# Contracting products of both feed-forward parts by seven block products, token block by token block

## The chip, the cores and the metric

The kernel runs on one core of one Trainium2 chip. The metric is device time in microseconds (us) of one execution; the time shown is the median of three runs. The profile is of one further execution. Engines are named as in the profile: PE (TensorE matmul), PEld (its weight load), DVE (VectorE), ACT (ScalarE), POOL (GpSimd), SP (SyncE, which here only issues DMAs).

## The reference, cut to what matters

Three different blocks follow one another on 1024 tokens of width 1024, all in float32. The second and the third end in a feed-forward part, and only these are touched:

```
# second block; inner width 22 * 128 = 2816
hn = rmsnorm_2(h, norm_ffn)
g, up = split(hn @ w_ffn_in)
h = h + (silu(g) * up) @ w_ffn_out
return rmsnorm_2(h, norm_final)

# third block; inner width 32 * 128 = 4096
m = rmsnorm_3(h, norm_mlp_g) @ w_mlp_up
h = h + square(relu(m)) @ w_mlp_down
return rmsnorm_3(h, norm_final_g)
```

The change concerns the products with `w_ffn_out` and `w_mlp_down`, which contract over the inner width. They are called the down products here, those with `w_ffn_in` and `w_mlp_up` the up products.

## The kernel before

Activations stand with the feature in the partitions and the 1024 tokens along the row, as two halves h of 512 tokens. A unit is 128 features by 1024 tokens, 512 KB. Every product is done in three passes, to keep float32 accuracy: a matrix is split into a high part in the matmul's own number type (a cast on ACT, L158, or L76 for a whole weight unit) and the remainder (a subtraction on DVE, L159 or L77), and the three matmuls of `mm3` (L149 to L151) add high by high, high by low and low by high in one PSUM bank.

The up products already go by seven block products in place of eight (`block_gemm`, Winograd's form of Strassen's method): P1 to P7 are matmuls (L358) of sums and differences of weight blocks, which POOL makes (L330 to L335), and of token blocks B11, B21, B22, T1 to T4, which stand ready in 28 split pages. `operand` prepares the weights of a product up to six products ahead. The inner activations go to DRAM (`hid_d`) unit by unit.

The down products are plain. `down_loads` loads residual rows (`ur`) and inner units (`hraw`) from DRAM by POOL's DMA queue and splits each unit into two pages; `gemm_out` then takes a group of 2 or 4 units, and for each of the 16 output halves (eight column blocks m of 128, two token halves h) runs 3 matmuls a unit into one PSUM bank (`mm`), which DVE adds onto the residual rows (`ev_add`, L1252 in the second block, L1646 in the third). Groups are `FF_GROUPS` in the second block, eight times 4 units in the third. The last group of each block runs in `seam` or `final`, which go on into the norm that follows.

Weights come in `Weights`: a unit of 512 KB is loaded by SP's queue into one of two raw buffers (`wraw`, L65), split as a whole (L76, L77) into one of four `wsplit` buffers.

The scheduler of the language puts every engine's instructions into one fixed order, by readiness and program order; each engine then runs its own queue in that order, and a waiting instruction holds all behind it. A tile's buffer is given out again when its last reader is done. There are 28 general pages of 128x1024 (`page`), a second pool of pages (`xpage`: 8 in the second block and 3 extra, 11 in the third), 4 half pages for intermediate results (`half_tmp`), and eight PSUM banks (`mm` 2, `tp` 2, `sc` 2 of two banks each).

## Time and profile before

| | |
|---|---|
| median of three runs | 3386.79 us (3385.83 to 3386.85) |
| the profiled execution | 3385.71 us, span 3383.9 us, granted clock 0.987 |
| PE busy | 3266.0 us, 97% of the span |
| DVE, ACT, POOL busy | 1937.2, 1169.3, 510.2 us: 57%, 35%, 15% |
| second block | the up part's block products (L358) begin at 1638.3 us; additions of the down part (L1252) 2020.1 to 2275.1 us |
| third block | block products (L358) end at 3013.3 us; additions of the down part 3018.8 to 3323.4 us (L1646), in `final` 3326.1 to 3372.1 us (L1722) |

Busy is the union of the durations of an engine's instructions. Matmuls overlap in their pipeline, so the duration in a row is longer than the distance from one start to the next. Some records are missing in the trace, so counts in a stretch are a little low. The clock is that which the chip granted PE, as a share of full speed.

### The profile page before, as it was taken

The page shows a single profiled execution, that of the slowest core. Times are in us where ns is not written, and L with a number is a line of the kernel's source. Part 1 is how long each engine was busy: PE and PEld are TensorE (multiplying, and loading weights), DVE is VectorE, ACT ScalarE, POOL GpSimd, SP SyncE. Part 2 cuts the span into 40 slices and gives each one's busy share as a digit, 9 for nine tenths or more (in the row PEclk, how much of TensorE's full clock was granted, in tenths as well). Part 3 has the DMA queues.
Part 4 walks back from the last instruction along what each step waited for, and adds up shares of the span by engine and source line. Part 5 has one row for each costly group of instructions (what it writes and reads, how often), then busy time and mean ns, then how long its engine had stood idle before and what let it go on. Part 6 is the DMA issues. An engine that isn't in the chain of part 4 may idle for free. (4 is left out here: it accounts for less than half of the span.)

```text
span 3383.9 us, 41750 instructions
## 1 busy us (share of the span) xinstructions
PE 3266.0 (97%) x16039; PEld 2666.3 (79%) x16039; DVE 1937.2 (57%) x3619; ACT 1169.3 (35%) x2115; POOL 510.2 (15%) x461
## 2 busy tenths in 40 slices
PE   6999999999999999999999999999999989999998
PEld 6788877677777888887788877878878778878887
DVE  7465566664755562446755566455569765554444
ACT  5222344433444442213433342134443433332211
POOL 0000000002200000102423220040211243220002
PEclk9999999999999999999999999999999999999999
DMA  5133211322211244422122244121112233362211
GB/s 188 58 103 127 87 57 38 113 69 78 72 46 42 70 147 159 143 94 103 66 84 85 81 179 148 57 97 54 46 51 75 103 103 109 112 251 94 69 50 56
DMA packets 128632, 318.52 MB, mean 94 GB/s; under 512 B 16305, under 2 KB 34865, under 8 KB 128433
## 3 DMA queue, kind: packets, MB, share of 16 engines
q1 hardware_dynamic: 104976, 236.63, 20.5%
q0 software_dynamic: 21440, 76.51, 6.4%
q8 instruction: 126, 2.06, 0.3%
q10 hardware_dynamic: 2016, 2.72, 0.2%
q14 instruction: 74, 0.60, 0.1%
HBM read 232.90 MB, written 82.90 MB: 93 GB/s over the span
## 5 line engine op out<-in xcount | busy, mean ns | idle before, releaser
L149 PE MATMUL mm<-sp,wsplit 128*128 128x512 f32 (+1 forms) x2880 | 1151.0, 400 | 30.0 <-ACT sp L158 9.7
L150 PE MATMUL mm<-sp,wsplit 128*128 128x512 f32 (+1 forms) x2880 | 1132.4, 393 | 9.5 <-DVE sp L159 7.1
L151 PE MATMUL mm<-sp,wsplit 128*128 128x512 f32 (+1 forms) x2880 | 1129.7, 392 | 0.0
L149 PEld LDWEIGHTS mm<-sp,wsplit 128*128 128x128 f32 x2880 | 547.1, 190 | 149.2 <-ACT sp L158 14.1
L150 PEld LDWEIGHTS mm<-sp,wsplit 128*128 128x128 f32 x2880 | 548.5, 190 | 117.3 <-DVE sp L159 10.2
L151 PEld LDWEIGHTS mm<-sp,wsplit 128*128 128x128 f32 x2880 | 547.7, 190 | 111.4 <-issue 0.4
L358 PE MATMUL mm<-sp,wsplit 128*128 128x512 f32 x1632 | 390.5, 391 | 6.6 <-ACT scp L362 5.0
L76 ACT CAST wsplit<-wraw 128x1024 fp32r<-128x1024 f32 x196 | 205.7, 1049 | 494.3 <-PE mm L151 468.3
L358 PEld LDWEIGHTS mm<-sp,wsplit 128*128 128x128 f32 x1632 | 306.5, 188 | 73.5 <-ACT scp L362 5.4
L77 DVE TENSOR_TENSOR wsplit<-wraw,wsplit 128x1024 fp32r<-128x1024 f32 x196 | 244.8, 1250 | 152.7 <-ACT wsplit L76 145.1
L358 PE MATMUL sc<-sp,wsplit 128*128 128x512 f32 x1224 | 296.6, 391 | 1.3 <-DVE c L372 1.3
L358 PEld LDWEIGHTS sc<-sp,wsplit 128*128 128x128 f32 x1224 | 231.1, 189 | 51.0 <-DVE c L372 1.7
L190 POOL TENSOR_TENSOR acc<-acc,sqt 128x512 f32<-128x512 f32 (+1 forms) x105 | 140.1, 1346 | 474.9 <-ACT sqt L189 388.3
L1646 DVE TENSOR_TENSOR ur<-ur,mm 128x512 f32<-128x512 f32 x112 | 76.8, 686 | 152.1 <-PE mm L151 152.1
L159 DVE TENSOR_TENSOR wsplit<-ssum,wsplit 128x512 fp32r<-128x512 f32 x136 | 101.8, 750 | 89.1 <-ACT wsplit L158 88.9
L1252 DVE SCALAR_TENSOR_TENSOR ur<-mm,ur 128x512 f32<-128x512 f32 x96 | 66.2, 689 | 106.5 <-PE mm L151 106.3
L158 ACT CAST wsplit<-ssum 128x512 fp32r<-128x512 f32 x136 | 82.9, 621 | 109.8 <-POOL ssum L335 36.0
L158 ACT CAST sp<-hraw 128x512 fp32r<-128x512 f32 x108 | 64.0, 620 | 65.2 <-PE mm L151 44.1
L333 POOL TENSOR_TENSOR ssum<-ssum,wraw 128x512 f32<-128x512 f32 x34 | 51.9, 1527 | 221.7 <-DVE wsplit L159 221.7
L158 ACT CAST wsplit<-wraw 128x512 fp32r<-128x512 f32 x102 | 61.8, 620 | 67.4 <-PE sc L358 47.8
L159 DVE TENSOR_TENSOR sp<-hraw,sp 128x512 fp32r<-128x512 f32 x108 | 71.3, 686 | 11.6 <-ACT sp L158 11.6
L335 POOL TENSOR_TENSOR ssum<-wraw,ssum 128x512 f32<-128x512 f32 x34 | 47.3, 1390 | 196.9 <-DVE wsplit L159 196.9
(550 smaller groups left out, 4234.2 us busy)
## 6 DMA issues: line engine op xcount, KB each, us to landing
wraw<-W SPq DMA_DIRECT2D x264, 512.0 KB, 3.7
hraw<-hid_d POOLq DMA_DIRECT2D x54, 512.0 KB, 6.0
hid_d<-scp SPq DMA_DIRECT2D x68, 256.0 KB, 2.0
t_d<-gl SPq DMA_DIRECT2D x32, 256.0 KB, 2.0
u<-x_d POOLq DMA_DIRECT2D x16, 512.0 KB, 6.0
gl<-t_d POOLq DMA_DIRECT2D x32, 256.0 KB, 3.1
u_d<-u SPq DMA_DIRECT2D x32, 256.0 KB, 2.0
ur<-u_d POOLq DMA_DIRECT2D x16, 512.0 KB, 8.2
```

The lines of the kernel that those rows point to most:

```text
L76: K.nc.scalar.copy(s[:, 0, :], r)
L77: K.nc.vector.tensor_sub(s[:, 1, :], r, s[:, 0, :].bitcast(F32))
L149: t.matmul(ps, wh, xh, start=first, stop=False)
L150: t.matmul(ps, wh, xl, start=False, stop=False)
L151: t.matmul(ps, wl, xh, start=False, stop=last)
L158: nc.scalar.copy(hi, src)
L159: nc.vector.tensor_sub(lo, src, hi.bitcast(F32))
L190: eng.tensor_add(acc, acc, t[:, :acc.shape[-1]])
L333: nc.gpsimd.tensor_sub(s, s, a11)
L358: nc.tensor.matmul(d, wk[:, c, :], xk[:, e, :], start=new and k == y == 0, stop=k == 3 and y == 2, skip_group_check=not new)
L1252: nc.vector.scalar_tensor_tensor(uu(m, h), ps, 0.5, uu(m, h), op0=OP.mult, op1=OP.add)
L1646: nc.vector.tensor_add(uu(m, h), uu(m, h), ps)
```

## The change

The down products go by seven block products too. `block_down` takes groups of 6 or 8 inner units. In a group the lower and the upper half of the units are the two inner blocks, the two token halves the two token blocks, and a pair of column blocks (2p and 2p + 1, p from 0 to 3) the two output blocks. Its seven stages P2, P1, P5, P6, P3, P7, P4 run one after the other, each for the four pairs, so that 28 slots make a group; a slot is n/2 units by three matmuls (L521). Token blocks of a stage are split two stages ahead; T1 and T2 are made by DVE, T3 and T4 by POOL. Weights of a slot are prepared up to six slots ahead from half units which SP loads (L437), with sums and differences on POOL (L451 to L457). Stages P2, P5 and P3 use four banks (two `tp`, two `mm`), the others the four banks of `sc`. A slot of P2, P3, P7 and P4 is added onto the residual by DVE (L530); a slot of P1, P5 and P6, whose result serves two outputs, is copied by ACT to a half page (`ut`, L528) and added by POOL (L532), and the PSUM bank goes on being summed into. The first 18 of 22 and 28 of 32 units go this way (`DOWN_2`, `DOWN_3`); the last four stay in `seam` and `final`. `then` begins the loads for the down part five products before the up part ends (`res_loads`, `inner_load`); the plain group's units are loaded and split 42 slots before the end (`inner_parts`). The weights are laid out anew in DRAM by the host (`down_units`), with no arithmetic.

```diff
-FF_GROUPS = (2, 4, 4, 4, 4, 4)
+
+DOWN_2, DOWN_3 = (6, 6, 6, 4), (8, 8, 6, 6, 4)
...
+
+    def skip(self, n):
+
+        self.given = self.split = self.loaded = self.given + n
+        self.end = self.n
...
+            if j == len(seq) - 5:
+                then()
...
+    def res_loads(self, u, u_d, page):
+
+        for k in (0, 2, 4, 6, 1, 3, 5, 7):
+            u[k] = page(name="ur")
+            self.nc.gpsimd.dma_start(u[k], u_d[k])
+            if k % 4 == 2 or k % 4 == 3:
                 yield
...
+    def inner_load(self, hid_d, ms):
+        raw = []
+        for m in ms:
+            raw.append(self.page(name="hraw"))
+            self.nc.gpsimd.dma_start(raw[-1], hid_d[m])
+        return raw
+
+    def inner_parts(self, hid_d, hid, ms):
+
+        raw = self.inner_load(hid_d, ms)
+        yield
+        for m, r in zip(ms, raw):
+            for h in (0, 1):
+                t = hid[m, h] = self.split_page()
+                self.split(t, 0, 512, r[:, h * 512:h * 512 + 512])
+            yield
+
+    def block_down(self, groups, u, hid_d, pools, scale):
+
+
+        nc = self.nc
+        stages = (("P2", "B21"), ("P1", "B11"), ("P5", "T1"), ("P6", "T2"), ("P3", "B22"), ("P7", "T3"), ("P4", "T4"))
+        seq = [(g, st, p) for g in range(len(groups)) for st in range(7) for p in range(4)]
+        first = [sum(groups[:g]) for g in range(len(groups))]
+        base = self.W.given
+        loads = dict(P2=("12",), P1=("11",), P5=("21", "22"), P6=("11",), P3=("12",), P7=("11", "21"), P4=("22",))
+        cols = lambda g: groups[g] * 64
+        order = [(j, b) for j, (g, st, p) in enumerate(seq) for b in loads[stages[st][0]]]
+        got, put = {}, [0]
+
+        def load_to(j):
+            while put[0] < len(order) and order[put[0]][0] <= j:
+                i, b = order[put[0]]
+                if put[0] % 2 == 0:
+                    pool, tag = pools[put[0] // 2 % len(pools)]
+                    self.half = pool.tile([128, 1024], F32, name="wraw", tag=tag)
+                g, _, p = seq[i]
+                w = cols(g)
+                t = self.half[:, put[0] % 2 * 512:put[0] % 2 * 512 + w]
+                nc.sync.dma_start(t, self.W.ap[base + 8 * g + 2 * p + int(b[0]) - 1][:, (int(b[1]) - 1) * w:int(b[1]) * w])
+                got[i, b] = t
+                put[0] += 1
+        sums, wt = {}, []
+
+        def operand(j):
+            g, st, p = seq[j]
+            w = cols(g)
+            q = stages[st][0]
+            x = [got.pop((j, b)) for b in loads[q]]
+            if q == "P5":
+                if p % 2 == 0:
+                    sums[p] = self.page(name="ssum")
+                    sums[p + 1] = sums[p][:, 512:]
+                nc.gpsimd.tensor_add(sums[p][:, :w], x[0], x[1])
+            elif q == "P6":
+                nc.gpsimd.tensor_sub(sums[p][:, :w], sums[p][:, :w], x[0])
+            elif q == "P3":
+                nc.gpsimd.tensor_sub(sums[p][:, :w], x[0], sums[p][:, :w])
+            elif q == "P7":
+                nc.gpsimd.tensor_sub(x[0], x[0], x[1])
+            if j % 2 == 0:
+                wt.append(self.ws.tile([128, 2, 1024], F32R, name="wsplit"))
+            self.split(wt[-1], j % 2 * 512, w, sums[p][:, :w] if q in ("P5", "P6", "P3") else x[0])
+            return wt[-1], j % 2 * 512
...
+        def fetch(g, high):
+            if g < len(groups):
+                n = groups[g] // 2
+                for k, t in enumerate(self.inner_load(hid_d, range(first[g] + n * high, first[g] + n * high + n))):
+                    X[g, high, k] = t
+
+        def block(g, st, k):
+            if st > 6:
+                g, st = g + 1, st - 7
+            if g >= len(groups) or k >= groups[g] // 2:
+                return
+            b = stages[st][1]
+            lo, hi = X[g, 0, k] if (g, 0, k) in X else None, X[g, 1, k]
+            x11, x12 = (lo[:, :512], lo[:, 512:]) if lo is not None else (None, None)
+            x21, x22 = hi[:, :512], hi[:, 512:]
+            if b == "T1":
+                nc.vector.tensor_sub(x11, x12, x11)
+            elif b == "T2":
+                nc.vector.tensor_sub(x11, x22, x11)
+            elif b == "T3":
+                nc.gpsimd.tensor_sub(x12, x22, x12)
+            elif b == "T4":
+                nc.gpsimd.tensor_sub(x21, x21, x11)
+            t = B[g, st, k] = self.split_page()
+            self.split(t, 0, 512, dict(B21=x21, B11=x11, T1=x11, T2=x11, B22=x22, T3=x12, T4=x21)[b])
+        fetch(0, 1)
+        fetch(0, 0)
+        load_to(9)
+        yield
+        for st in (0, 1):
+            for k in range(4):
+                block(0, st, k)
+        a, f, ready = {}, {}, []
+        for j, (g, st, p) in enumerate(seq):
+            q = stages[st][0]
+            load_to(j + 10)
+            while len(ready) < min(j + 6, len(seq)):
+                ready.append(operand(len(ready)))
+            if p == 0 and st == 2:
+                fetch(g + 1, 1)
+            if p == 0 and st == 4:
+                fetch(g + 1, 0)
+            block(g, st + 2, p)
+            if q == "P2":
+                f[p] = (self.tp, self.tp, self.mm, self.mm)[p]()
+            elif q == "P1" and p % 2 == 0:
+                t = self.sc()
+                a[p], a[p + 1] = t[:, :512], t[:, 512:]
+            d = f[p] if q in ("P2", "P5", "P3") else a[p]
+            new = q in ("P2", "P1", "P5")
+            w, o = ready[j]
+            n = groups[g] // 2
             for k in range(n):
-                raw.append(pages[1](name="hraw"))
-                nc.gpsimd.dma_start(raw[k], hid_d[m + k])
-                yield
-            for k in range(n):
-                for h in (0, 1):
-                    t = self.split_page()
-                    self.split(t, 0, 512, raw[k][:, h * 512:h * 512 + 512])
-                    hid[m + k, h] = t
-                yield
-            m += n
+                xk = B[g, st, k]
+                wk = w[:, :, o + k * 128:o + k * 128 + 128]
+                for y, (c, e) in enumerate(((0, 0), (0, 1), (1, 0))):
+                    nc.tensor.matmul(d, wk[:, c, :], xk[:, e, :], start=new and k == y == 0, stop=k == n - 1 and y == 2,
+                                     skip_group_check=not new)
+            m, h = dict(P2=(0, 0), P1=(0, 0), P5=(1, 1), P6=(0, 1), P3=(0, 1), P7=(1, 1), P4=(1, 0))[q]
+            r = u[2 * p + m][:, h * 512:h * 512 + 512]
+            with self.tc.high_priority(offset=PRIO_E):
+                if q in ("P1", "P5", "P6"):
+                    t = self.half_tmp("ut")
+                    nc.scalar.activation(t, d, AF.Copy, scale=scale)
+                else:
+                    nc.vector.scalar_tensor_tensor(r, d, scale, r, op0=OP.mult, op1=OP.add)
+            if q in ("P1", "P5", "P6"):
+                nc.gpsimd.tensor_add(r, r, t)
+            yield
...
-        for _ in self.block_gemm(20, B, page, out):
+        hid = {}
+        n = sum(DOWN_2[:-1])
+        self.W.end = self.W.given + 40
+        down = self.block_down(DOWN_2[:-1], u2, hid_d, ((self.wr, "wraw"), (self.wr, "wraw")) + ((extra, "px"),) * 3, 0.5)
+
+        rl = []
+
+        def then():
+            next(down)
+            rl.append(self.spawn(self.res_loads(u2, u2_d, self.xpage)))
+        for _ in self.block_gemm(20, B, page, out, then):
             self.tick()
+        self.finish(*rl)
+        for i, _ in enumerate(down):
+            self.tick()
+            if i == 28 * len(DOWN_2) - 28 - 42:
+                self.W.skip(8 * len(DOWN_2) - 8)
+                mg = self.spawn(self.meta_norm())
+                dl = self.spawn(self.inner_parts(hid_d, hid, range(n, 22)))
+        self.finish(mg, dl)
+        self.x2_d = self.dr.tile([9, 128, 1024], F32, name="x2_d")
+        r = self.seam(u2, lambda k, h: hid[n + k, h], DOWN_2[-1], ev_add, "norm_final_2", "norm_mix_g_3", self.x2_d)
         px.close()
...
+        n = sum(DOWN_3[:-1])
+        self.W.end = self.W.given + 28
+        down = self.block_down(DOWN_3[:-1], u3, hid_d, ((self.wr, "wraw"), (self.wr, "wraw")) + ((self.px, "px"),) * 3, 1.0)
+
+        rl = []
+
+        def then():
+            next(down)
+            rl.append(self.spawn(self.res_loads(u3, u3_d, self.xpage)))
+        for _ in self.block_gemm(14, B, page, out, then):
             self.tick()
-        self.down = 0
-        self.spawn(self.down_loads(u3, u3_d, (self.page, self.xpage), hid, hid_d, (4,) * 8))
-        for gi in range(8):
-            m0 = 4 * gi
-            src3 = lambda k, h, m0=m0: hid[m0 + k, h]
-            self.down = gi
-            while (m0 + 3, 1) not in hid:
-                self.tick()
-            if gi < 7:
-                for _ in self.gemm_out(src3, 4, ev_add):
-                    self.tick()
-            else:
-                self.final(u3, src3)
+        self.finish(*rl)
+        for i, _ in enumerate(down):
+            self.tick()
+            if i == 28 * len(DOWN_3) - 28 - 42:
+                self.W.skip(8 * len(DOWN_3) - 8)
+                dl = self.spawn(self.inner_parts(hid_d, hid, range(n, 32)))
+        self.finish(dl)
+        self.final(u3, lambda k, h: hid[n + k, h])
...
+def down_units(w, groups):
+
+    out, o = [], 0
+    for i, n in enumerate(groups):
+        g = w[128 * o:128 * (o + n)]
+        o += n
+        if i + 1 < len(groups):
+            u = g.reshape(n, 128, 8, 128).transpose(2, 1, 0, 3).reshape(8, 128, n * 128)
+            out.append(np.concatenate([u, np.zeros((8, 128, 1024 - n * 128), w.dtype)], axis=2))
```

Two places show how the order of instructions moves. The first is POOL's queue in the second block, where the up part ends and the down part begins. `hraw` is a unit of inner activations, `ur` a residual row block; the rows with the names mtm, lrug and mtt load constants of the third block. Before:

```order
L335 TENSOR_TENSOR ssum<-wraw,ssum 128x512
L394 DMA hraw<-hid_d 128x1024 x2
L390 DMA ur<-u_d 128x1024 x6
L394 DMA hraw<-hid_d 128x1024 x2
L390 DMA ur<-u_d 128x1024
L394 DMA hraw<-hid_d 128x1024 x2
L1495 DMA mtm<-metat 16x512 x2
```

Now (`ssum` is a weight sum, `ut` a copied product):

```order
L342 TENSOR_TENSOR ssum<-wraw,ssum 128x512
L402 DMA hraw<-hid_d 128x1024 x6
L394 DMA ur<-u_d 128x1024 x7
L451 TENSOR_TENSOR ssum<-wraw 128x384 x3
L485 TENSOR_TENSOR hraw<-hraw 128x512 x3
L487 TENSOR_TENSOR hraw<-hraw 128x512
L451 TENSOR_TENSOR ssum<-wraw 128x384
L487 TENSOR_TENSOR hraw<-hraw 128x512
L394 DMA ur<-u_d 128x1024
L453 TENSOR_TENSOR ssum<-ssum,wraw 128x384 x2
L402 DMA hraw<-hid_d 128x1024 x3
L532 TENSOR_TENSOR ur<-ur,ut 128x512
```

The residual loads now come behind the first six units, and sums and differences stand between the loads where POOL had loads alone.

The second place is DVE's queue inside a down part of the second block. `sp` is a split page, `wsplit` a weight split; L1252 and L530 are additions of a PSUM bank onto the residual, L481 makes T1. Before, one split of a whole weight unit follows every four additions:

```order
L1252 SCALAR_TENSOR_TENSOR ur<-mm,ur 128x512 x4
L77 TENSOR_TENSOR wsplit<-wraw,wsplit 128x1024
L1252 SCALAR_TENSOR_TENSOR ur<-mm,ur 128x512 x4
L77 TENSOR_TENSOR wsplit<-wraw,wsplit 128x1024
L1252 SCALAR_TENSOR_TENSOR ur<-mm,ur 128x512 x2
L159 TENSOR_TENSOR sp<-hraw,sp 128x512 x3
L1252 SCALAR_TENSOR_TENSOR ur<-mm,ur 128x512
```

Now, in the first group, from the end of its first stage on:

```order
L530 SCALAR_TENSOR_TENSOR ur<-mm,ur 128x512
L166 TENSOR_TENSOR wsplit<-ssum,wsplit 128x384 x2
L166 TENSOR_TENSOR sp<-hraw,sp 128x512 x5
L166 TENSOR_TENSOR wsplit<-ssum,wsplit 128x384 x2
L166 TENSOR_TENSOR sp<-hraw,sp 128x512
L166 TENSOR_TENSOR wsplit<-ssum,wsplit 128x384 x4
L166 TENSOR_TENSOR sp<-hraw,sp 128x512 x5
L166 TENSOR_TENSOR wsplit<-ssum,wsplit 128x384 x2
L166 TENSOR_TENSOR sp<-hraw,sp 128x512 x4
L481 TENSOR_TENSOR hraw<-hraw 128x512 x2
```

Before, most of the rows take one operand from PSUM; now nearly all take both from SBUF.

## Rows read from the trace of the kernel before

**Rows 1.** The page, part 1: busy us, share of the span, instructions.

```profile
PE 3266.0 (97%) x16039; PEld 2666.3 (79%) x16039; DVE 1937.2 (57%) x3619; ACT 1169.3 (35%) x2115; POOL 510.2 (15%) x461
```

**Rows 2.** Stretches: us, busy time (instructions) by engine, granted clock, DMA share, GB/s.

```profile
1700.00:2000.00 300.00, 300.00 (x1325) 248.43 (x1324) 155.52 (x222) 106.82 (x190) 91.76 (x69) 1.00 0.25 83
2000.00:2050.00 50.00, 45.75 (x189) 35.94 (x189) 41.24 (x88) 26.50 (x46) 10.46 (x20) 0.97 0.87 328
2060.00:2240.00 180.00, 180.00 (x795) 148.78 (x795) 76.67 (x109) 31.99 (x43) 11.25 (x12) 1.00 0.20 69
3000.00:3050.00 50.00, 46.35 (x191) 37.66 (x190) 27.45 (x38) 13.56 (x21) 9.59 (x19) 0.93 0.78 307
```

**Rows 3.** Timeline of PE: start us, duration us, merged instructions.

```profile
2002.99 5.60 PE L358 MATMUL mm<-sp,wsplit 128*128 128x512 f32 x24
2008.43 2.88 PE L358 MATMUL sc<-sp,wsplit 128*128 128x512 f32 x12
```

**Rows 4.** Timeline of POOL, 1727 to 1733 us.

```profile
1728.96 1.30 POOL L330 TENSOR_TENSOR ssum<-wraw 128x512 f32<-128x512 f32 x1
1730.21 1.74 POOL L331 TENSOR_TENSOR ssum<-wraw,wraw 128x512 f32<-128x512 f32 x1
```

**Rows 5.** Timeline of DVE, 1727 to 1733.2 us.

```profile
1729.69 1.12 DVE L159 TENSOR_TENSOR wsplit<-ssum,wsplit 128x512 fp32r<-128x512 f32 x1 [0.53 <-ACT wsplit L158]
1730.73 1.78 DVE L1314 SCALAR_TENSOR_TENSOR c<-silu,c 128x512 f32<-128x512 f32 x1
1732.43 0.68 DVE L159 TENSOR_TENSOR wsplit<-wraw,wsplit 128x512 fp32r<-128x512 f32 x1
1733.04 0.68 DVE L159 TENSOR_TENSOR wsplit<-ssum,wsplit 128x512 fp32r<-128x512 f32 x1
```

**Rows 6.** Groups by form of POOL, 1700 to 2000 us: busy us, mean ns, idle before.

```profile
L390 POOL DMA_DIRECT2D ur<-u_d x5 | 2.6, 528 | 0.0
```

**Rows 7.** Groups of DVE, 2060 to 2240 us.

```profile
L77 DVE TENSOR_TENSOR wsplit<-wraw,wsplit 128x1024 fp32r<-128x1024 f32 x16 | 19.6, 1224 | 4.9 <-ACT wsplit L76 4.9
L159 DVE TENSOR_TENSOR sp<-hraw,sp 128x512 fp32r<-128x512 f32 x16 | 10.6, 685 | 2.0 <-ACT sp L158 2.0
```

**Rows 8.** Groups by form of DVE, 1700 to 2000 us.

```profile
L1314 DVE SCALAR_TENSOR_TENSOR c<-silu,c 128x512 f32<-128x512 f32 x16 | 18.6, 1163 | 0.8 <-ACT silu L1313 0.8
...
L372 DVE TENSOR_TENSOR c<-c,sc 128x512 f32<-128x512 f32 x16 | 11.0, 688 | 29.1 <-PE sc L358 29.1
```

**Rows 9.** Timeline of POOL, 2705 to 2713 us.

```profile
2706.43 7.03 POOL L295 TENSOR_TENSOR u<-u,u 128x512 f32<-128x512 f32 x1 [23.66 <-ACT sp L158]
```

**Rows 10.** Source line 190: duration ns min/median/max, first and last start, forms.

```profile
L190 POOL TENSOR_TENSOR acc<-acc,sqt x105: 721/1292/2260, 821.7 to 3373.1; 128x512 f32<-128x512 f32 x91, 128x256 f32<-128x256 f32 x14
```

**Rows 11.** Timeline of DVE, 2705 to 2713 us (first and last of five merged rows).

```profile
2705.60 0.68 DVE L294 TENSOR_TENSOR u<-u 128x512 f32<-128x512 f32 x1
...
2710.42 1.89 DVE L159 TENSOR_TENSOR sp<-u,sp 128x512 fp32r<-128x512 f32 x3
```

**Rows 12.** Timeline of PE, 2999 to 3027 us (in brackets: idle before, releaser).

```profile
3018.25 0.80 PE L149 MATMUL mm<-sp,wsplit 128*128 128x512 f32 x1 [3.65 <-ACT hd L1679]
3018.84 0.63 PE L150 MATMUL mm<-sp,wsplit 128*128 128x512 f32 x1
...
3024.39 0.41 PE L151 MATMUL mm<-sp,wsplit 128*128 128x512 f32 x1
```

**Rows 13.** Timeline of ACT, 3012 to 3019 us.

```profile
3014.49 1.14 ACT L158 CAST sp<-hraw 128x512 fp32r<-128x512 f32 x2 [4.56 <-DMA hraw<-hid_d]
```

**Rows 14.** The page, part 6: DMA issues, KB each, median us to landing.

```profile
wraw<-W SPq DMA_DIRECT2D x264, 512.0 KB, 3.7
hraw<-hid_d POOLq DMA_DIRECT2D x54, 512.0 KB, 6.0
```

**Rows 15.** Groups of ACT, 2060 to 2240 us.

```profile
L158 ACT CAST sp<-hraw 128x512 fp32r<-128x512 f32 x16 | 9.2, 619 | 11.2 <-PE mm L151 10.8
```

More of the change, by code (lines that the diff above doesn't have):

```diff
@@ L87, in take @@
         return [self.raw.pop(j + i) for i in range(n)]
+    def skip(self, n):
+        self.given = self.split = self.loaded = self.given + n
+        self.end = self.n
     def get(self, ahead=1):
@@ L309, in block_tokens, with block_gemm @@
                     yield
-    def block_gemm(self, n, B, page, out):
+    def block_gemm(self, n, B, page, out, then):
         nc = self.nc
@@ L2088, in pack @@
     up, dn = fm_units(f("w_mlp_up_3")[0]), f("w_mlp_down_3")[0]
-    W.append(up)
-    W += [t4_units(dn[512 * i:512 * i + 512]) for i in range(8)]
+    W += [up] + down_units(dn, DOWN_3)
     mt = f("meta_tokens_3")
```

41 lines of the change are left out of this document (6 added, 35 removed).

## The prediction

> **What bounds the kernel now.** I read the page's busy shares first: TensorE (PE) is busy 97% of the span, VectorE (DVE) 57%, ScalarE (ACT) 35%, GpSimd (POOL) 15% [rows 1]. An average says little about one stage, so the next view is the table of stretches [rows 2]. The up products of the second block (1700 to 2000 us) and its plain down product (2060 to 2240 us) both show PE busy for the whole stretch at a granted clock of 1.00; only the stretches in which the up part goes over into the down part (2000 to 2050 and 3000 to 3050 us) lose something: PE busy 45.75 and 46.35 of 50 us, clock 0.97 and 0.93. So in the stage that is changed, PE alone sets the time. The other engines have room there: in the plain down stretch DVE 76.67, ACT 31.99 and POOL 11.25 of 180 us. That room is what the change spends.
>
> The price of a matmul is not its row's duration (0.39 us, pipelined) but the distance of starts: 24 products of 128x512 start at 2002.99 us and the next group at 2008.43 us, so 5.44 / 24 = 0.2267 us each [rows 3].
>
> **The change, part by part.** *Matmuls.* The plain down product costs 48 matmuls a unit of 128 inner rows (16 output halves, three passes): 22 x 48 = 1056 in block two, 32 x 48 = 1536 in block three. A group of n units in blocks costs 7 products x 4 column pairs x n/2 x 3 = 42 n. Units 6+6+6 and 8+8+6+6 go this way: 756 + 1176 = 1932; the last 4 units of each block stay plain, 2 x 192. So 2592 - 1932 - 384 = 276 matmuls go: 276 x 0.2267 = **-62.6 us**, if PE stays fed.
>
> *What feeds it.* A block product needs sums and differences that the plain one does not. Counted in the program, over both blocks: VectorE gets 140 weight splits of 128x384 and 56 of 128x512, 161 splits of inner blocks, 46 token differences (T1, T2), and 112 evictions that add a PSUM bank to the residual; GpSimd gets 80 sums of 128x384 and 32 of 128x512, 46 differences (T3, T4), 84 adds onto the residual. All this falls into 1932 x 0.2267 = 438 us of PE time. Each engine alone has time for its share. VectorE: 263 x 0.61 + 140 x 0.46 + 112 x 0.61 = 293 us. GpSimd: 162 x 1.25 + 80 x 0.94 = 278 us, beside 70 DMA issues of 0.53 us [rows 6], 37 us. (0.61 and 1.25 are distances of starts back to back, 1732.43 to 1733.04 and 1728.96 to 1730.21 us [rows 4, 5]; a width of 384 is put at three quarters, an estimate from VectorE's 1024 and 512 wide splits, 1224 and 685 ns [rows 7].)
>
> *Do the two run side by side?* Here the trace speaks against the change. In one stretch a GpSimd sum ends at 1728.96 + 1.30 = 1730.26; the VectorE split that started at 1729.69 ends at 1730.81, 0.55 later; the next GpSimd sum, started at 1730.21, ends only at 1731.95, 1.14 after that; the next VectorE operation, started at 1730.73, ends at 1732.51, 0.56 later [rows 4, 5]. They take turns. Operations with one input in PSUM do not: L372 (PSUM added to SBUF) keeps 688 ns in the mean, while L1314 of the same shape with both inputs in SBUF takes 1163 ns [rows 8]. And the turn is not fair: one GpSimd difference took 7.03 us instead of 1.29, from 2706.43 to 2713.46 [rows 9, 10], while VectorE ran two-input operations back to back from 2705.60 to 2712.31 [rows 11]. The Trainium skill, page "SBUF — State Buffer", section "Who interferes with whom", states the same thing as a rule: a VectorE instruction with two SBUF inputs and a GpSimd instruction that reads SBUF need one read port, the second is blocked, for the whole instruction. By the rows a turn lasts 0.55 and 1.14 us, less than the instructions.
>
> So the two engines' times add, except for the 112 evictions. By turns as in [rows 4, 5] (0.41 and 0.86 us at 384): VectorE 263 x 0.55 + 140 x 0.41 = 202 us, GpSimd 162 x 1.14 + 80 x 0.86 = 253.5 us, sum 455.6 us: 17.6 more than PE's 438. By distances of starts, with nothing saved where one hands over to the other: 224.8 + 277.7 = 502.5 us, 64.5 more. To both come 16 splits for the two closing plain groups, 9.8 us by 0.61; from both goes what is done ahead, about 8 us at the start of each part (operands run up to six products ahead, 12 us, less what the last up products still need), 16 us. So PE waits between **+11 and +58 us**. I take **+35**, the middle: the rows show both kinds of hand-over, and groups of 6 (57.1 us of PE for 61 to 67 us of turns) cannot borrow from groups of 8 (76.2 for 76 to 84).
>
> *The seam from up to down.* Now the seams lose 4.25 + 3.65 us idle and, by the clock, 0.03 x 50 + 0.07 x 50 = 5 us: 12.9 us [rows 2]. At 3018.25 us PE had waited 3.65 us for an eviction (L1679) that stood behind casts in ACT's queue; ACT had waited 4.56 us for a load of inner rows [rows 12, 13]. Then PE ran at the lower clock level: 13 distances of starts from 3018.84 to 3024.39 us, 0.43 us each [rows 12]. The change starts these loads five products, 13.6 us, before the up part ends, with the residual rows behind them. I take back 8 of the 12.9 us: **-8**; bounds are 0 (loads of 6.0 us in the median [rows 14] still land late in the burst) and -12.9.
>
> *Costed at nothing.* ACT: 161 + 196 casts and 84 copies at 0.62 us or less [rows 15] are at most 273 of 438 us, and no row shows it taking turns. DMA: the weights of the block part come as 252 loads of 192 or 256 KB through ten half slots; a 512 KB load lands in 3.7 us [rows 14], and a slot comes round in 10 / 252 x 438 = 17 us. If that cover went (a slot held while GpSimd lags), one load of 3.7 us per group, 7 in all, would cost 26 us. POOL's queue: each load of inner rows waits there for a free page, and residual adds and weight sums stand behind it; the six to eight loads of a group are hidden as long as their pages were read long ago; a page that PE still reads would hold the adds and sums behind it for a product or two, 2 to 5 us a group, which the upper half of the range takes in.
>
> *Sum.* The profiled execution took 3385.7 us (span 3383.9). 3385.7 - 62.6 - 8 + 35 = 3350.1. The median of the runs lies 1.1 us above the profiled one: **3351 us**.
>
> **Rivals.** *The turns cost nothing* (sums run far enough ahead, GpSimd fits between VectorE's operations as in the up part, where PE stays full with POOL at 91.76 and DVE at 155.52 of 300 us [rows 2]). For it: the order of the changed program lets GpSimd run some ten products ahead. Against: by the same turns the up part, with 10 two-input VectorE operations and 4 GpSimd sums in seven products, fills (10 x 0.55 + 4 x 1.14) / (84 x 0.2267) = 53% of the time, this part 104% or more. Time: 3386.8 - 62.6 - 8 = 3316 us.
>
> *Slower: a turn lasts as long as the row says.* Then VectorE holds 263 x 0.685 + 140 x 0.55 = 257 us and GpSimd 162 x 1.29 + 80 x 1.00 = 289 us (1.00 lies between 0.721 at 256 and 1.292 at 512 wide [rows 10]): 546 us, 108 over PE; with 11 for the closing splits and 16 done ahead, 103 us of waiting. Time: 3386.8 - 62.6 - 8 + 103 = 3419 us. It decides from 71 us of waiting on, 10 us a group. By its words this is how the rule of the Trainium skill's page "SBUF — State Buffer" would come out. The alternating rows speak against it: a pair took 1.69 us there, not 1.98. For something like it speaks the 7.03 us row: a starved GpSimd holds up adds whose four buffers ACT needs, then ACT's casts, and the port stands idle.
>
> *The clock falls.* After the idle 3.65 us those 13 distances cost 13 x (0.43 - 0.227) = 2.6 us [rows 12]. One such gap in each of seven groups is 18 us: 3369 us. Short waits spread out need not do this. It is within the range.
>
> **How the numbers follow.** Turns at +11 to +58 with the seams and an occasional clock drop: 0.66, 3322 to 3382 us. Turns free: 0.18, 3311 to 3322. Turns by full rows or starvation: 0.11, 3382 and up. The rest, 0.05, lies about no change. The range that leaves out no more than 2 in 10 is 3314 to 3388. A measurement of this kernel tells some 0.2% (7 us) from no change: faster than 3380.0 takes the first two cases without a little of the first's end, 0.84; within 0.2%, 0.07; slower, 0.09.
>
> **What would show it.** Right: 276 matmuls fewer; the down parts (438 us of PE) last 460 to 495 us, with PE waiting mostly for wsplit of VectorE and ScalarE and these for ssum of GpSimd; POOL busy 65 to 95% there, its sums longer than 1.3 us, VectorE's splits longer than 0.69; groups of 6 lose more per matmul than groups of 8; almost no wait at the seams. Wrong: PE full through the groups (turns free), or PE waiting mainly for DMA, for PSUM evictions or for pages, or the granted clock well below 0.95 in the groups.

## The result and the profile after

| | before | after |
|---|---|---|
| median | 3386.82 us (3385.83 to 3390.0) | 3449.53 us (3447.6 to 3453.38) |
| profiled span, granted clock | 3383.9 us, 0.987 | 3445.9 us, 0.974 |

Both medians are of four runs. The change makes the kernel slower: ratio 1.0179, with a 95% interval of [1.0165, 1.0194], which is 62.7 us. The forecast of 3351 us was wrong in sign.

Part 1 of the page after (busy us, share of the span, instructions), which answers to [rows 1]:

```profile
PE 3234.6 (94%) x15763; PEld 2626.7 (76%) x15763; DVE 2175.6 (63%) x3802; ACT 1295.7 (38%) x2416; POOL 862.3 (25%) x703
```

The 276 matmuls are gone (16039 to 15763), and yet the span grew. The table of stretches of the kernel after (us, busy time and instructions by engine, granted clock, DMA share, GB/s) shows where. The first row is an up part, the second and the fourth are the whole down parts of the second and the third block:

```profile
1700.00:2000.00 300.00, 300.00 (x1325) 248.51 (x1324) 155.08 (x222) 107.51 (x192) 91.51 (x71) 1.00 0.26 87
2012.40:2245.40 233.00, 193.64 (x770) 152.43 (x769) 205.74 (x263) 94.35 (x189) 152.58 (x124) 0.90 0.42 138
...
2125.00:2150.00 25.00, 14.50 (x52) 11.12 (x51) 24.11 (x19) 12.01 (x23) 20.92 (x18) 0.80 0.39 122
3032.10:3385.90 353.80, 293.66 (x1193) 233.90 (x1192) 288.38 (x306) 138.69 (x256) 222.94 (x166) 0.91 0.40 134
```

The up part is what it was in [rows 2]. The down parts take 233.0 + 353.8 = 586.8 us for 1963 matmuls, which at 0.2267 us are 445.0 us. PE stands idle for 39.4 + 60.1 = 99.5 us; the other 42 us are matmuls at the lower clock level and the pipeline's run-out ahead of each gap. At the lower level the distance of starts is 0.43 us, as in [rows 12]; 132 distances of 0.40 to 0.46 us stand behind PE's gaps, 26 us more than the same number at 0.2267. From 2125 to 2150 us PE has work in 14.5 of 25 us, at a granted clock of 0.80.

What ended PE's waits in the third block's down part (us in all, times, longest):

```profile
PE sc L521 <- ACT ut L528: 44.5, 8, 9.5
PE sc L521 <- DVE ur L530: 15.6, 6, 5.8
```

PE waits for PSUM banks, not for weights: the copy of a bank to `ut` comes late. One such wait, step by step. DVE (start, duration, idle before in brackets):

```profile
2052.54 7.67 DVE L166 TENSOR_TENSOR sp<-hraw,sp 128x512 fp32r<-128x512 f32 x1
```

POOL beside it:

```profile
2052.15 0.58 POOL L402 DMA_DIRECT2D hraw<-hid_d  x1
2052.75 1.27 POOL L532 TENSOR_TENSOR ur<-ur,ut 128x512 f32<-128x512 f32 x1
2053.97 1.97 POOL L457 TENSOR_TENSOR wraw<-wraw 128x384 f32<-128x384 f32 x2
2055.89 3.76 POOL L532 TENSOR_TENSOR ur<-ur,ut 128x512 f32<-128x512 f32 x3
```

ACT and PE behind them:

```profile
2060.24 1.66 ACT L165 CAST sp<-hraw 128x512 fp32r<-128x512 f32 x3 [6.48 <-DVE sp L166]
2061.81 0.59 ACT L528 ACTIVATE ut<-sc 128x512 f32<-128x512 f32 x1
```

```profile
2063.76 3.92 PE L521 MATMUL sc<-sp,wsplit 128*128 128x512 f32 x9 [3.99 <-ACT ut L528]
```

A split that takes 0.69 us in [rows 7] takes 7.67 here, while POOL runs six operations. ACT's next cast waits 6.48 us for it, the copy of the bank stands behind that cast in ACT's queue, and PE waits 3.99 us for the bank. Elsewhere the two engines go one by one. Three DVE operations took 5.13 us, 1.71 each, beside POOL rows of 1.7 us:

```profile
3082.32 5.13 DVE L166 TENSOR_TENSOR sp<-hraw,sp 128x512 fp32r<-128x512 f32 x3
```

```profile
3081.81 1.73 POOL L457 TENSOR_TENSOR wraw<-wraw 128x512 f32<-128x512 f32 x1
3083.50 1.73 POOL L455 TENSOR_TENSOR ssum<-wraw,ssum 128x512 f32<-128x512 f32 x1
```

Over the third block's down part the groups by form of DVE and POOL (busy us, mean ns, idle before) read:

```profile
L166 DVE TENSOR_TENSOR sp<-hraw,sp 128x512 fp32r<-128x512 f32 x98 | 106.1, 1115 | 11.7 <-ACT sp L165 11.6
L166 DVE TENSOR_TENSOR wsplit<-ssum,wsplit 128x512 fp32r<-128x512 f32 x24 | 38.9, 1652 | 4.2 <-ACT wsplit L165 4.1
...
L530 DVE SCALAR_TENSOR_TENSOR ur<-sc,ur 128x512 f32<-128x512 f32 x31 | 21.2, 686 | 21.8 <-PE sc L521 21.8
```

```profile
L532 POOL TENSOR_TENSOR ur<-ur,ut 128x512 f32<-128x512 f32 x48 | 72.0, 1508 | 13.6 <-ACT ut L528 13.4
L485 POOL TENSOR_TENSOR hraw<-hraw 128x512 f32<-128x512 f32 x14 | 30.3, 2171 | 24.2 <-DVE hraw L481 24.2
```

DVE's splits of these two groups grew from 0.69 us to 1.1 and 1.65 us; its evictions, with one input in PSUM, kept 0.686.

POOL and SP wait as well. From the view of waits of the same part, POOL's longest and that of SP's queue:

```profile
POOL ssum L451 <- DMA wraw<-W: 28.8, 8, 7.8
SPq L437 <- DVE wsplit L166: 116.1, 28, 18.7
```

The weight sums wait for weight loads, and SP cannot issue these before DVE's splits (and POOL's own sums) have read the half slots that they go to. In both parts together POOL waits 71 us for weight loads.

### The profile page after: what moved, and what is told of

It is laid out like the page before. It is cut to its first block, busy times and chain, and to the rows that moved or that the text cites. A ratio compares the mean times of both kernels' runs of the same rounds, so it can differ in the third digit from the quotient of the medians.

```text
span 3445.9 us, 42361 instructions
## 1 busy us (share of the span) xinstructions
PE 3234.6 (94%) x15763; PEld 2626.7 (76%) x15763; DVE 2175.6 (63%) x3802; ACT 1295.7 (38%) x2416; POOL 862.3 (25%) x703
## 4 chain that ended last, share of the span: by engine, by line
PE 73%; DVE 14%; issue 4%; POOL 4%; ACT 3%; DMA 2%; SPq 0%; POOLq 0%; DVEq 0%; ACTq 0%
PE mm L156 13%; PE mm L157 13%; PE mm L158 13%; PE mm L367 10%; PE sc L367 7%; PE sc L521 4%; DVE sp L166 3%; DVE wsplit L166 3%; DMA wraw<-W 2%; PE mm L1938 1%; PE sc L1200 1%; DVE wsplit L79 1%; PE tp L156 1%; POOL ur L532 1%; PE tp L157 1%
## 5 line engine op out<-in xcount | busy, mean ns | idle before, releaser
L156 PE MATMUL mm<-sp,wsplit 128*128 128x512 f32 (+1 forms) x2144 | 859.3, 401 | 23.6 <-ACT sp L165 9.6
L157 PE MATMUL mm<-sp,wsplit 128*128 128x512 f32 (+1 forms) x2144 | 842.8, 393 | 9.5 <-DVE sp L166 7.1
L158 PE MATMUL mm<-sp,wsplit 128*128 128x512 f32 (+1 forms) x2144 | 840.7, 392 | 0.0
L156 PEld LDWEIGHTS mm<-sp,wsplit 128*128 128x128 f32 x2144 | 406.5, 190 | 111.7 <-ACT sp L165 13.1
L157 PEld LDWEIGHTS mm<-sp,wsplit 128*128 128x128 f32 x2144 | 407.6, 190 | 88.5 <-DVE sp L166 10.4
L158 PEld LDWEIGHTS mm<-sp,wsplit 128*128 128x128 f32 x2144 | 407.2, 190 | 81.5 <-issue 0.4
L521 PE MATMUL sc<-sp,wsplit 128*128 128x512 f32 x1104 | 298.1, 428 | 99.1 <-ACT ut L528 72.2
L367 PEld LDWEIGHTS mm<-sp,wsplit 128*128 128x128 f32 x1632 | 306.5, 188 | 72.7 <-ACT scp L371 5.4
L521 PEld LDWEIGHTS sc<-sp,wsplit 128*128 128x128 f32 x1104 | 225.4, 209 | 165.7 <-ACT ut L528 81.4
L367 PE MATMUL sc<-sp,wsplit 128*128 128x512 f32 x1224 | 296.5, 391 | 0.1
L166 DVE TENSOR_TENSOR wsplit<-ssum,wsplit 128x512 fp32r<-128x512 f32 (+1 forms) x220 | 220.5, 1017 | 110.9 <-ACT wsplit L165 110.6
L367 PEld LDWEIGHTS sc<-sp,wsplit 128*128 128x128 f32 x1224 | 231.0, 189 | 49.8 <-DVE c L381 0.8
L166 DVE TENSOR_TENSOR sp<-hraw,sp 128x512 fp32r<-128x512 f32 x177 | 184.9, 1079 | 19.6 <-ACT sp L165 19.1
L165 ACT CAST wsplit<-wraw 128x512 fp32r<-128x512 f32 (+1 forms) x214 | 117.2, 579 | 179.6 <-issue 56.1
L165 ACT CAST wsplit<-ssum 128x512 fp32r<-128x512 f32 (+1 forms) x220 | 125.4, 590 | 157.3 <-POOL ssum L342 36.1
L166 DVE TENSOR_TENSOR wsplit<-wraw,wsplit 128x512 fp32r<-128x512 f32 (+1 forms) x214 | 161.3, 772 | 15.5 <-ACT wsplit L165 12.6
L532 POOL TENSOR_TENSOR ur<-ur,ut 128x512 f32<-128x512 f32 x84 | 126.1, 1512 | 23.5 <-ACT ut L528 23.1
```

What stands on the lines that cost most here:

```text
L156: t.matmul(ps, wh, xh, start=first, stop=False)
L157: t.matmul(ps, wh, xl, start=False, stop=False)
L158: t.matmul(ps, wl, xh, start=False, stop=last)
L165: nc.scalar.copy(hi, src)
L166: nc.vector.tensor_sub(lo, src, hi.bitcast(F32))
L367: nc.tensor.matmul(d, wk[:, c, :], xk[:, e, :], start=new and k == y == 0, stop=k == 3 and y == 2, skip_group_check=not new)
```

## The experiments

Four theories stood against each other. **A:** DVE and POOL share a way to SBUF, so every POOL operation takes time from DVE, which feeds PE. **B:** the copies to `ut` are the fault (their place in ACT's queue, or their ring of four half pages). **C** and **D:** POOL's sums simply come late (by loads, or because POOL is slow), and no port matters. A later one, **E,** came out of the trace. Brackets are 95% intervals of the ratio to the kernel before, run beside each of these; its median was 3386.1 to 3388.9 us there, so a difference between two runs is good to a few us.

### Taking work from POOL, step by step

The first edit gives all slots the eviction that P2, P3, P7 and P4 had:

```diff
-                if q in ("P1", "P5", "P6"):
-                    t = self.half_tmp("ut")
-                    nc.scalar.activation(t, d, AF.Copy, scale=scale)
-                else:
-                    nc.vector.scalar_tensor_tensor(r, d, scale, r, op0=OP.mult, op1=OP.add)
-            if q in ("P1", "P5", "P6"):
-                nc.gpsimd.tensor_add(r, r, t)
+                nc.vector.scalar_tensor_tensor(r, d, scale, r, op0=OP.mult, op1=OP.add)
```

> Edit: a slot of P1, P5 and P6 is added onto the residual by VectorE straight from its PSUM bank, as the other slots are; ScalarE's copy and GpSimd's addition (84 each) are gone. Theory A (VectorE and GpSimd keep each other from SBUF, whole chains at a time): GpSimd loses 84 of its 242 operations, about 96 us of turns, VectorE gets 84 additions of some 0.61 us that take no turn; of the 136 us that TensorE lost in the down parts some 70 to 100 come back: 3350 to 3380 us. Theory B (the copies stand late in ScalarE's queue, and the four half pages they go to are given back late): the same edit takes the cause away altogether, 3330 to 3360 us, and it then makes no difference who makes the sums. Theory C (the weight sums come too late whatever else is done, by loads or by GpSimd's own pace): within 15 us of 3450.

3417.12 us, 1.0088 [1.0073, 1.0103] of before: 32.4 us back, 0.39 us for each POOL operation taken away. That is less than A said, much less than B and more than C. PE still waits for banks, and with the copies gone the wait is put down to DVE's additions alone, in place of 72.2 us for the copies and 26.6 for the additions over the whole changed kernel:

```profile
PE sc L521 <- DVE ur L526: 70.3, 23, 10.4
```

The second takes T3 and T4 too (two lines, `nc.gpsimd.tensor_sub` to `nc.vector.tensor_sub`):

> Edit: as the run above, and the token differences T3 and T4 (46) are made by VectorE. GpSimd is left with the 112 weight sums. Theory A: VectorE's load rises to about 372 of 438 us, but the port's does not: 46 turns of 1.14 us become 46 of 0.55, 27 us less; 10 to 30 us faster than with the additions alone. Theory B: no difference from the additions alone, or a few us slower by VectorE's load. Theory C: no difference.

3384.36 us, 0.9989 [0.998, 0.9999]: another 32.8 us, 0.71 for each difference; a little more than A's range, where B and C had no gain.

The third takes the weight sums as well:

```diff
-                nc.gpsimd.tensor_add(sums[p][:, :w], x[0], x[1])
+                nc.vector.tensor_add(sums[p][:, :w], x[0], x[1])
...
-                nc.gpsimd.tensor_sub(x[0], x[0], x[1])
+                nc.vector.tensor_sub(x[0], x[0], x[1])
```

> Edit: as the run above, and the weight sums on VectorE too: GpSimd only issues loads in the down parts. No two engines share a port any more, but VectorE has about 428 of 438 us to do. Theory A: the waits that are left come from VectorE's own pace; it lies within 20 us of the run before on either side, and GpSimd's absence shows in VectorE's splits at 0.69 us or less everywhere. Theory B: slower than the run before by 20 to 60 us, since evictions now stand behind still more work in VectorE's queue. Theory C: faster if GpSimd's pace was the cause, unchanged if the loads were.

**3323.0 us, 0.9809 [0.9795, 0.9824]:** 61.4 us more, and a version that beats both kernels. A had the direction of the splits' durations right and the size wrong: it put this step at 20 us either way. B had it slower. C, in the form that POOL's pace is the fault, had it faster too, so this step alone does not decide between the port and lateness. Its stretches, the two down parts whole:

```profile
2014.20:2196.70 182.50, 177.72 (x770) 143.15 (x769) 177.25 (x338) 75.35 (x151) 10.61 (x20) 1.00 0.53 175
2985.10:3258.50 273.40, 271.20 (x1188) 221.53 (x1187) 261.22 (x446) 113.40 (x208) 13.65 (x26) 1.00 0.53 173
```

And one of DVE's groups in the second of them:

```profile
L166 DVE TENSOR_TENSOR sp<-hraw,sp 128x512 fp32r<-128x512 f32 x98 | 65.1, 684 | 0.1
```

DVE carries out all that POOL did and is busy 438.5 us in the two parts, where it was busy 494.1 us with POOL's help. These splits are back at 0.684 us. PE waits 7.0 us in 455.9.

### Is it the port, or POOL's lateness?

To the kernel with everything on DVE, 112 sums that nobody needs were added on POOL; `z` is a scratch page, and the copy of one column keeps each sum near its old time:

```diff
             self.split(wt[-1], j % 2 * 512, w, sums[p][:, :w] if q in ("P5", "P6", "P3") else x[0])
+            if q in ("P5", "P6", "P3", "P7"):
+                nc.gpsimd.tensor_copy(z[:, 0:1], wt[-1][:, 0, j % 2 * 512:j % 2 * 512 + 1].bitcast(F32))
+                nc.gpsimd.tensor_add(z[:, 512:512 + w], z[:, :w], z[:, :w])
```

> Edit to the kernel with all sums, differences and additions on VectorE: GpSimd makes 112 further sums of the old shapes on a scratch page, each behind a read of one column of the weight split's cast, so that it comes when the old ones came; no other engine waits for them. Theory A (port): as slow as the kernel whose weight sums GpSimd made, 3384, give or take 20: 3365 to 3405 us. Theory D (not the port: GpSimd's sums come late because its operations are slow and stand in a chain of waits): 3323 to 3330 us, no change.

3381.69 us, 0.9978 [0.9968, 0.9987]: 58.7 us lost to sums without a reader. DVE's splits of the third block's part rose:

```profile
L166 DVE TENSOR_TENSOR sp<-hraw,sp 128x512 fp32r<-128x512 f32 x100 | 74.3, 762 | 0.1
...
L166 DVE TENSOR_TENSOR wsplit<-ssum,wsplit 128x512 fp32r<-128x512 f32 x24 | 22.6, 958 | 0.0
```

The control replaces the sum by `nc.gpsimd.memset(z[:, 512:512 + w], 0.0)`:

> As the run above, but each further sum on GpSimd is a fill (memset) of the same shape, which reads nothing from SBUF; the read of one column is kept. Theory A in the form that only reading operations share the port: 3323 to 3332 us. Theory A in the form that any GpSimd access to SBUF does: between 3332 and the run above, by the fills' duration. Theory D: 3323 to 3330.

3332.07 us, 0.9829 [0.9815, 0.9844], on the border of A's two forms. The fills did not stand where the sums had stood, though. A sum reads the copied column and so keeps its place; nothing ties a fill to it, and in the trace all 112 run ahead, from 2017 to 2050 and from 2993 to 3039 us, while the column copies keep their places. So this run prices page, copies and early fills at 9 us together, and shows fills beside DVE's work only in those two stretches: 28 splits of 512 columns had a fill beside them for over 0.2 us there, and none took longer than 0.692 us. In the whole part the splits are as short as without POOL:

```profile
L166 DVE TENSOR_TENSOR sp<-hraw,sp 128x512 fp32r<-128x512 f32 x100 | 66.5, 685 | 0.1
```

The difference to the run above, 49.6 us or 0.44 us a sum, is what the sums in their places cost. DVE does the same work in both, and its busy time (the third number with a count) shows where the time goes. The third block's down part with sums, then with fills:

```profile
3007.00:3317.70 310.70, 284.31 (x1189) 227.67 (x1188) 293.95 (x446) 113.97 (x208) 110.32 (x154) 0.97 0.46 153
2992.10:3268.30 276.20, 272.66 (x1188) 222.69 (x1187) 261.40 (x446) 113.91 (x208) 68.77 (x154) 0.99 0.52 172
```

Over both parts DVE is busy 491.2 us in the run with sums and 440.1 in the run with fills, 51 us more, and PE waits 38.7 us for DVE's additions in place of 7.1. The fills, being early, do not test lateness; D falls for these sums because no operation uses what they make, and ACT, the only engine that waited for POOL's reads, did so for 3.6 us in all. C falls with it, since DVE and ACT waited no more than 12 us for weight loads in either run.

### The copies

> Edit to the kernel with everything on VectorE: the slots of P1, P5 and P6 are again copied by ScalarE to half pages first, and VectorE adds the copy onto the residual; GpSimd still has nothing to do. Theory B (the copies' place in ScalarE's queue costs the time): 30 us or more slower than 3323. Theory A: 0 to 10 us slower, since no port is shared; VectorE's own load is the same.

```diff
+                if q in ("P1", "P5", "P6"):
+                    t = self.half_tmp("ut")
+                    nc.scalar.activation(t, d, AF.Copy, scale=scale)
...
+                nc.vector.tensor_add(r, r, t)
```

3325.42 us, 0.9815 [0.9798, 0.9831]: 2.4 us beside the kernel with everything on DVE, within both runs' spread: with POOL idle the copies in ACT's queue cost nothing that can be told from noise. Beside a busy POOL they could be taken away and PE's waits moved to DVE's additions (70.3 us, above). So the releaser that the view of waits names, ACT's copy, carried the delay and did not make it. The ring was tried on the changed kernel itself (`t = up[:, p % 2 * 512:...]`, with `up` a general page for two slots):

> Edit to the changed kernel: the copies of P1, P5 and P6 go to halves of general pages in place of the ring of four half pages; nothing else. Theory A: the residual additions may lag further without stopping ScalarE, but the port's load is the same: 0 to 25 us faster than 3450. Theory B in its form that the ring of four is too short: 60 us or more faster. Theory C: no change.

3464.96 us, 1.0227 [1.0212, 1.0242]: slower by 15 us. B falls in both forms. A, which had put this at 0 to 25 us faster, and C, with no change, missed it too; why it is slower no run shows.

### The port by itself

> The port by itself: the kernel's work is left out, its outputs are written with other data. Seven stretches one after the other: (1) 16 VectorE differences 128x512, both inputs in SBUF, alone; (2) 8 GpSimd sums 128x512 alone; (3) both chains together, VectorE's operands ready first; (4) both, GpSimd's ready first; (5) as 3 with one VectorE input in PSUM; (6) 16 of VectorE beside 16 fills (memset) on GpSimd, which read nothing; (7) 12 VectorE differences, each behind a cast on ScalarE, beside 8 GpSimd sums. Turn theory (as I predicted: one operation each in turn): in 3 and 4 the engines alternate, 8 pairs of 1.69 to 1.98 us and then the other 8 of VectorE; the longest operation under 2 us. Chain theory (who has it keeps it while its own queue goes on without a break): in 3 VectorE's 16 end in some 10 us as if alone and GpSimd's first sum shows 8 to 10 us; in 4 VectorE's first shows 8 to 10 us. Both: 5 and 6 run side by side, each at its own pace. In 7 the turn theory gives pairs, the chain theory GpSimd back to back first and a first difference of several us.

Both chains alternated whichever was ready first: DVE 16 operations alone in 11.59 us, POOL 8 alone in 10.65; together a pair every 1.67 us. Rows of the third stretch:

```profile
32.40 3.26 POOL L2285 TENSOR_TENSOR R<-P,Q 128x512 f32<-128x512 f32 x2
32.91 1.63 DVE L2284 TENSOR_TENSOR F<-D,E 128x512 f32<-128x512 f32 x1
```

With one input in PSUM, from the groups of that run, and against fills, from its timeline, DVE kept 0.69 us:

```profile
L2286 DVE TENSOR_TENSOR F<-X,E 128x512 f32<-128x512 f32 x16 | 11.1, 691 | 2.3 <-ACT D L2281 1.8
```

```profile
87.26 0.69 DVE L2284 TENSOR_TENSOR F<-D,E 128x512 f32<-128x512 f32 x1 [3.03 <-ACT E L2283]
```

The turn theory held; the chain theory, which the 7.67 us row had suggested, did not. The last stretch told nothing, since most of its casts came after POOL's chain.

> The port by itself again, the kernel's work left out. In the first such run every chain wrote one tile, so that each operation waited for the one before it (0.03 us on VectorE, 0.08 on GpSimd) and the engines alternated, 1.67 us a pair. Here the operations of a chain write tiles of their own and follow without a gap, as in the kernel. Stretches: both chains gapless with VectorE ready first; the same with GpSimd ready first; GpSimd with gaps; VectorE with gaps; VectorE with one PSUM input; GpSimd gapless with a copy of one column after each sum. Chain theory: gapless GpSimd ready first makes VectorE's first operation last some 8 x 1.25 = 10 us, and gaps on the side that has the port bring the pairs of 1.67 us back. Turn theory: pairs of 1.67 us or so in all, no operation over 2 us, and the 6 to 8 us rows of the kernel have another cause (a semaphore that the row hides).

Gapless chains alternate too, again 1.67 us a pair; DVE alone needs 0.60 from start to start. The chain theory fell. What then makes rows of 7.67 us? In the changed kernel 12 DVE rows in the down parts last over 2.5 us, 56.3 us together, and eight of them begin while POOL issues a load (that of 7.67 us at 2052.54 us, inside the issue of 2052.15 to 2052.73); the other four, up to 5.62 us, do not.

> The port by itself, a third time, the kernel's work left out. In the second such run VectorE and GpSimd alternated in every phase, a pair in 1.67 us, so that chains alone do not starve anyone; but most of the VectorE rows of over 2.5 us in the changed kernel begin while GpSimd issues a DMA. Eight stretches: GpSimd issues a load and then runs six sums without a gap, while VectorE runs four differences whose operands come ready at four different times during and after the issue; then four stretches without the load. Theory E (an operation of VectorE that begins beside a DMA issue on GpSimd loses its turn until GpSimd's chain ends): in one or more of the first four stretches the first difference lasts some 6 to 8 us, in none of the last four. Turn theory: pairs of 1.67 us in all eight, and the long rows stay unexplained.

Here theory E was right about the mechanism, and more sharply than put. A summary of DVE's differences (ns min/median/max), stretches with a load and without:

```profile
L2294 DVE TENSOR_TENSOR F<-D,E x16: 677/678/8325, 8.2 to 59.7; 128x512 f32<-128x512 f32 x16
...
L2294 DVE TENSOR_TENSOR F<-D,E x16: 959/1744/1747, 64.1 to 107.2; 128x512 f32<-128x512 f32 x16
```

In each of the four stretches with a load one difference lasted 7.9 to 8.3 us, until POOL's six sums were done; one of these began 0.06 us after the issue had ended. Without a load none passed 1.75 us. Does the kernel pay for it? In the next run `q` is SyncE's queue from the second group on:

```diff
-            self.nc.gpsimd.dma_start(raw[-1], hid_d[m])
+            (q or self.nc.gpsimd).dma_start(raw[-1], hid_d[m])
```

> Edit to the changed kernel: the inner units of all groups but the first are loaded by SyncE's queue in place of GpSimd's; nothing else. Theory E: with no DMA issues in GpSimd's queue inside the groups VectorE's rows of over 2.5 us (12 in the down parts, about 56 us in all) go, and with them the longest waits of TensorE: 3400 to 3430 us. Turn theory without it: 3440 to 3455. Against both, slower than 3455: a load that waits for a page holds the weight loads behind it on SyncE's queue.

3451.08 us, 1.0187 [1.017, 1.0204]: no change. The DVE rows over 2.5 us fell from 12 to 3, 17.3 us together, and the time stayed. E's forecast of the time falls. Its price is not settled by that, for the edit cost something elsewhere: POOL waited 94 us for weight loads in the down parts, where it had waited 71. It may also be that what a starved DVE loses POOL gains, with 1.25 us a sum in place of 1.7; no run separates the two.

### The seam

On the kernel with everything on DVE, `j == len(seq) - 5` became `j == len(seq) - 1`.

> Edit to the kernel with everything on VectorE: the loads for the down part begin at the up part's last product and not five products ahead of its end. My prediction's term for the seam was 8 us for both, bounds 0 and 12.9. If it holds: 6 to 13 us slower than 3323, with TensorE waiting for loads of inner units at both seams. If the early start is worth nothing: 3320 to 3326.

3325.01 us, 0.9813 [0.9796, 0.9829]: no difference, but the trace shows that the edit tested nothing. The scheduler put the loads where they had been: the third block's first inner units are issued 26.3 us before the down part's first matmul in both kernels, and POOL's queue has the same order there. With the start five products ahead:

```profile
2958.82 2.14 POOL L402 DMA_DIRECT2D hraw<-hid_d  x4
2985.14 2.00 PE L521 MATMUL tp<-sp,wsplit 128*128 128x512 f32 x8
```

With the start at the last product:

```profile
2961.20 2.14 POOL L402 DMA_DIRECT2D hraw<-hid_d  x4
2987.53 2.00 PE L521 MATMUL tp<-sp,wsplit 128*128 128x512 f32 x8
```

So the run is a second measurement of the kernel with everything on DVE, 2 us from the first. Its stretches about the two seams:

```profile
2000.00:2050.00 50.00, 49.05 (x215) 39.97 (x214) 45.73 (x83) 22.74 (x46) 9.92 (x19) 1.00 0.86 316
2980.00:3040.00 60.00, 60.00 (x266) 49.30 (x265) 58.75 (x97) 26.64 (x48) 6.49 (x13) 1.00 0.77 271
```

PE is all but full at the seams, at clock 1.00, where [rows 2] had 45.75 of 50 us at 0.97 and 46.35 at 0.93.

## Why the prediction was wrong

**Matmuls, -62.6: right.** The 276 are gone, and where the feed holds the kernel is 3386.8 - 3323.0 = 63.8 us faster; the other terms nearly cancel there, as the next paragraph shows.

**Seam, -8: the size within its bounds where POOL has no arithmetic, the cause not tested.** With everything on DVE the two stretches lose 0.84 us where before lost 12.9. Whether the early loads save it no run shows, since the edit that should have delayed them did not. The traces fit it: in the third block the first inner unit was issued 18 us before the up part's last matmul ended, behind four residual loads; now it is 31 us, ahead of all residual loads (the prediction had 13.6). That kernel's down parts take 455.9 us for 1958 matmuls, 12 us more than 1958 x 0.2267, 7 of them waits of PE. So 62.6 and about 12 are gained, about 12 are lost again, and some 63 are left. In the changed kernel itself the saving does not show: from 2000 to 2050 us PE is busy 44.77 us at clock 0.97, about as before.

**Feed, +35: the step that failed.** From 3449.5 = 3386.8 - 62.6 - 8 + x the waiting is x = 133 us in place of 35. Of these, 126.5 go when POOL has no arithmetic left. For the weight sums (112 of POOL's 242 operations, 61.4 us) the sums without a reader show that sharing SBUF with DVE is enough to cost nearly as much; for the additions and differences (65.2 us) there is no such control, and the same cause is argued from their rows. Three parts of the step can be told apart.

*The turn was right.* A pair was put at 1.69 us and measured 1.67, alone and in the kernel (1.71). The prediction's slower rival, full rows of 1.98, was wrong in its mechanism, and its 3419 us too low. But its case, 3382 us and up at a chance of 0.11, is the one that came, and its last sentence was nearest to what happened: an engine starved, ACT's casts held up, the port idle. It had GpSimd as the starved one; in the rows above it was VectorE.

*The port's time was right at its upper end.* From the starts and ends of all rows in the two down parts, DVE (other than its evictions) or POOL's arithmetic was running for 203.2 + 298.9 = 502 us. The upper bound had 502.5, "with nothing saved where one hands over"; taking the middle threw away some 23 us. (With the closing splits and what is done ahead the upper bound was 496.)

*That the port would never rest was the error.* The bounds set the port's time against PE's 438 us as if one or the other were always at work. In the 586.8 us the port was unused for 85: 38 us in which DVE evicted and POOL did nothing (I had called the evictions free, beside POOL; of their 75 us POOL ran beside 30), and 47 us in which neither computed. Of the 586.8 - 445.0 = 142 us lost in the down parts 57 are port time over PE's time, which the range covered, and 85 are this rest, which no term had. The 47 are queues that wait for each other: for 27 of them DVE's next operation was an addition that waited for PE to finish a bank, and for 21 POOL's next was a weight sum or difference that waited for its load, whose slots DVE and POOL had still to read (the view of SP above).

**The clock, a rival at 18 us:** the mechanism was right (the granted clock was 0.90 and 0.91 in the two parts), the size was more: 26 us by the distances at the lower level, 42 at most. There were 23 waits for banks in the two parts and not 7, the longest 10.2 us. It is part of the 133.

**Costed at nothing.** ACT's copies cost 2.4 us beside an idle POOL, and moving the loads out of POOL's queue brought no net change. The weight loads were not covered: POOL waited 71 us for them. The prediction had named this chain ("a slot held while GpSimd lags") and put it at 26 us, outside the sum. With everything on DVE and the same ten half slots its weight sums wait 2.7 us for loads, so the late loads follow from the lag; what they add to it is open, since no run gave them more slots. That DVE would be *less* busy without help was in no part of the sum.

**The signs.** Down parts of 460 to 495 us: wrong, 586.8. PE waiting for splits of DVE and ACT: wrong, it waited for evictions, which I had named as a sign against me; the experiment with the copies shows that this view named the carrier. POOL at 63 and 65% with its loads, its 512 wide sums over 1.3 us and DVE's splits over 0.69: right. Groups of 6 losing more than groups of 8: wrong; the first group of each block loses most (0.356 and 0.341 us a matmul over 252 and 336, worked out from the first and the last start; the later ones 0.259 to 0.310). Why the first ones do is not settled by any run; in the kernel with everything on DVE all groups lie between 0.228 and 0.243. Nor is it settled which queue begins each of the waits in the 47 us.

## What to carry to other kernels

Before work is moved from VectorE to GpSimd to relieve it, look for VectorE operations with both inputs in SBUF beside it: here such a pair took 1.67 us, while VectorE needed 0.60 us to do the sum itself, so the help cost more than the work. Work without a reader tells contention from lateness: 112 dummy sums cost 58.7 us, while the waits for their reads came to 3.6. In the changed kernel the view of waits named ACT's copies, which cost 2.4 us when put back beside an idle GpSimd. And a sum of turns on something two engines share is a lower bound of the time, not an upper one, unless one of them always has work ready.

## What the hardware showed beyond that

An operation of VectorE with two SBUF inputs that began during GpSimd's issue of a DMA, or just behind it, did not get its turn until GpSimd's whole chain was done: 7.9 to 8.3 us over six sums, four times of four, where the same chains without the issue alternate at 1.67 us. That one input in PSUM (0.691 us mean), or fills on GpSimd (0.69 us), leave VectorE alone is as the Trainium skill has it on its page "SBUF — State Buffer", section "Who interferes with whom": by it a VectorE instruction with at most one SBUF input, outside the two-port modes, does not contend, and one with two contends with a GpSimd instruction that reads SBUF but not with one that only writes it. The runs agree.
